# Output projection in sixteen half-depth passes, and scans by token half: a hybrid attention and delta-rule layer on one core

## The chip, the cores and the metric

The kernel runs on one core of one Trainium2 chip. The metric is the device time of one execution in microseconds. Several executions are timed and their median is used; one further execution is profiled, and all rows of the trace come from that one.

## What is computed

One layer over 1024 tokens of width 2048, in float32. The normalised input goes through one wide projection. Its columns feed eight heads of differential attention (A) and eight heads of a gated delta rule (B). The outputs of both are put side by side, multiplied by one more weight matrix, added to the input and normalised.

```python
h = rms_norm(x, norm_w)
proj = jnp.einsum('btd,dc->btc', h, w_in)
...
o_da = differential_attention(q1, q2, k1, k2, v_da, lam, rel_bias)
...
def step(S, inp):                      # one chunk of tokens of one head
    qc, kc, uc, wc, qkc, gc, glc = inp
    v_new = uc - jnp.einsum('bhcd,bhdv->bhcv', wc, S)
    o = (jnp.einsum('bhcd,bhdv->bhcv', qc * jnp.exp(gc)[..., None], S)
         + jnp.einsum('bhij,bhjv->bhiv', qkc, v_new))
    S = (S * jnp.exp(glc)[..., None, None]
         + jnp.einsum('bhcd,bhcv->bhdv', kc * jnp.exp(glc[..., None] - gc)[..., None], v_new))
    return S, o
...
mixed = jnp.concatenate([o_da, o_gdn], axis=-1)          # (1024, 2048)
x = x + jnp.einsum('btc,cd->btd', mixed, w_out)
return rms_norm(x, final_norm_w)
```

## The kernel before, in words

**Order of the work.** The program is written as coroutines ("lanes"), each of which yields one instruction at a time. A planner asks all lanes for their next instruction, works out with fixed costs when each could start, and emits the one that could start earliest; of equal ones the lane that stands first in the list wins. What comes out is one fixed order of instructions per engine and one fixed order of transfers on SyncE's queue (SP). A lane can also yield a condition, and then it stands still until the planner has emitted what the condition asks for. All instructions are issued by one helper, so the profile gives line 369 for nearly all of them (401 for transfers), and groups are told apart by tile names.

**Stages.** The input projection runs first, and attention beside it. When attention's last unit is done (`("attend", H - 1, 3)`), two things begin together: the scans of the delta rule, and the output projection.

**Scans.** There are 16: eight heads by two token halves of 512. `scan_loads` fetches six operands per scan (kT, qT, qk, Um in parts, vr, kh) into three sets of buffers; a set is loaded again when the scan that used it has ended. Two lanes, `scans(0)` and `scans(1)`, take the even and the odd heads. A scan has four steps of 128 tokens, each a chain through three engines: matmul with the state S, VectorE makes R, matmul with Um, ScalarE makes vn, matmul with kh, VectorE makes the next S. It uses four PSUM banks, `bka` and `bkb`, two for each lane. At its end it is normalised, turned, and stored to `mixed[1]` in DRAM. Before the change a lane takes a head's first half, then the same head's second half, then its next head.

**Output projection.** `mixed` has 16 blocks of 128 channels: 8 of attention (`mixed[0]`) and 8 of the scans (`mixed[1]`). The loop `out_products` goes over passes, a pass being one token half (four blocks of 128 tokens) by 512 output columns. Before the change there are eight, and each takes all 16 blocks of channels: for each pair of blocks j, and each block k and token block tb in it, three matmuls of 128x512 (operands are split into a high and a low part in fp32r, and high x high, low x high and high x low are summed). That is 192 matmuls into four PSUM banks. Even passes use the banks `prod` (two), `side` and `av`; odd passes use the scans' banks and ask for all scans to be done (`scans_done()`).

**Operands of the projection.** They live in the buffers of the input projection, which come free as its last products are issued (`FREE`). `out_weights` loads w_out 1 MB at a time (four blocks of channels by 512 columns) into `B11h` and `B11l` and splits it in two parts into the slots `RING_W`; `out_left` loads 1 MB of `mixed` at a time through `T1h` and splits it into the slots `RING_A`. For ScalarE and VectorE (or GpSimd) a part is one copy and one subtraction of 128x1024.

**Rows of the result.** `acc_loads` loads x in eight row blocks, three in tiles named `raw`, the fourth in `acc`; blocks 4 to 7 take the same four places when blocks 0 to 3 are stored (`("stored", n - 4)`). `collect_out` adds the four banks of a pass to them on VectorE. `half_row` normalises and stores a row block; it needs `fnw`, the final norm's weights, which `last_room` loads when all scans are done.

Of the kernel before, what the change touches and what calls it, by code (L numbers as in the profile page):

```python
# [11 lines left out]
F32 = mybir.dt.float32  # L12
# [11 lines left out]
D = 2048  # L24
H = 8
P = 128
# [440 lines left out]
@with_exitstack  # L467
def hybrid_trunk(ctx: ExitStack, tc: tile.TileContext, a, out):
    nc = tc.nc
    plan = Planner(tc, ("s_rest", "s_narrow", "s_blocks", "s_turn", "follow", "follow_b", "s_ts", "drain", "scores", "tails", "outputs", "s_norm", "s_scales", "weights", "s_nsum", "s_sums", "s_scale", "keys", "lead", "norms", "side_w", "products"))  # L470
    s_rest, s_narrow, s_blocks, s_turn, follow, follow_b, s_ts, drain, scores_, tails, outputs, s_norm, s_scales, weights_, s_nsum, s_sums, s_scale, keys, lead, norms, a_lane, main = plan.lanes
    pe, act, dve, pool = plan.engines
    dma = plan.dma

# [44 lines left out]
    done = set()  # L519
    box = {}  # L520

    def when(*keys):
        return lambda: all(k in done for k in keys)
# [30 lines left out]
    def bank_of(lane):  # L554
        return ps.tile([P, 512], F32, ("bka", "bkb")[lane], 2)
# [1017 lines left out]
    def scan_loads():  # L1573
        yield when(("attend", H - 1, 3))
        box["ast"].close()
        plan.margin = lambda: 0.0
        box["gst"] = ExitStack()
        gp = box["gp"] = rpool(box["gst"], "gp")
        for h0 in range(0, H, 2):
            for h, g in ((h0, 0), (h0 + 1, 0), (h0, 1), (h0 + 1, 1)):  # L1580
                yield when(("gq", h, g), ("gv", h, g))
                yield lambda: len(ring) < SETS or ring[-SETS][0]
                flag = [False]
                ring.append(flag)
                cs = slice(4 * g, 4 * g + 4)
                kT = gp.tile([P, 512], F32, "kT", SETS)
                dma(kT, kd[h][:, hsl(g)])
                qT = gp.tile([P, 512], F32, "qT", SETS)
                dma(qT, gq[h][:, hsl(g)])
                qk = gp.tile([P, 4, P], F32, "qk", SETS)  # L1590
                dma(qk, ed[h][:, cs])
                U = gp.tile([P, 4, P], F32, "Um", SETS)
                yield pool.memset(U[64:128, :, 0:64], 0.0)
                for s in range(2):
                    dma(U[64 * s:64 * s + 64, :, 64 * s:64 * s + 64], ud[h, cs, s].rearrange("c j i -> j c i"))
                dma(U[0:64, :, 64:128], u12d[h][:, cs])
                vr = gp.tile([P, 4, P], F32, "vr", SETS)
                dma(vr, gv[h][:, cs])
                kh = gp.tile([P, 4, P], F32, "kh", SETS)
                dma(kh, khd[h][:, cs])  # L1600
                ahead[h, g] = kT, qT, qk, U, vr, kh, flag

    def scans(lane):
        ends = None
        for h, g in [(h, g) for h in range(lane, H, 2) for g in range(2)]:
            ends = yield from scan(lane, h, g, ends)
        yield from ends

    def scan(lane, h, g, ends):
# [12 lines left out]
        o = vr  # L1622
        S = last_s.get(h)
        for k in range(4):
# [17 lines left out]
            if c < NT - 1:  # L1642
                p4 = bank_of(lane)
                yield pe.matmul(p4[:, :P], kh[:, k], vn, start=True, stop=True)
                Sn = gp.tile([P, P], F32, f"S{lane}", 2)
                if c:
                    yield dve.scalar_tensor_tensor(out=Sn, in0=S, scalar=egl[:, h, c:c + 1], in1=p4[:, :P],
                                                   op0=ALU.mult, op1=ALU.add)
                else:
                    yield dve.tensor_copy(Sn, p4[:, :P])  # L1650
                S = Sn
# [70 lines left out]


    wo_v = w_out.rearrange("(a p) d -> p a d", p=P)
    RAW_W, RAW_A = ("B11h", "B11l"), ("T1h",)
    RING_W = ("T2h", "T2l", "T3h", "T3l")
    RING_A = ("T1l", "B21h", "B21l", "T4h", "T4l", "B22h", "B22l", "x0", "x1")
    FREE = {n + e: LAST - 6 + i for i, (_, n) in enumerate(ORDER) for e in "hl"}
    PASSES = [(half, q) for half in range(2) for q in range(4)]
    NP = len(PASSES)  # L1730
    ops, used, acc = {}, set(), {}
    passed = [0]

    def scans_done():
        return all(("scan", h, g) in done for h in range(H) for g in range(2))
# [9 lines left out]
    def slot(tag, shape, dt):  # L1745
        if tag in FREE:
            yield lambda: issued[0] >= FREE[tag]
        else:
            yield lambda: "fp" in box
        return (hp if tag in FREE else box["fp"]).tile(shape, dt, tag)  # L1750

    def raw_rows(n, names, src):

        t = yield from slot(names[n % len(names)], [P, 4, 512], F32)
        dma(t, src)
        return t

    def parts(key, names, raw):

# [7 lines left out]
        ops[key] = t[:, 0], t[:, 1]  # L1767

    def out_weights():
        raws = {}  # L1770

        def fetch(n):
            if n < NP * 4:
                p, j = divmod(n, 4)
                q = PASSES[p][1]
                raws[n] = yield from raw_rows(n, RAW_W, wo_v[:, 4 * j:4 * j + 4, q * 512:(q + 1) * 512])

        for n in range(len(RAW_W)):
            yield from fetch(n)
        for n in range(NP * 4):  # L1780
            for i in range(2):
                yield from parts(("w", 2 * n + i), RING_W, raws[n][:, 2 * i:2 * i + 2])
            yield from fetch(n + len(RAW_W))

    def out_left():
        for n in range(8):
            half, j = divmod(n, 4)
            chunk, k = divmod(4 * j, NH)
            if chunk:
                yield when(*(("scan", k + i, half) for i in range(4)))  # L1790
            else:
                yield when(*(("attend", k + i, 2 * half + m) for i in range(4) for m in range(2)))
            raw = yield from raw_rows(n, RAW_A, mixed[chunk][:, k:k + 4, half * 512:(half + 1) * 512])
            for i in range(2):
                yield from parts(("a", 2 * n + i), RING_A, raw[:, 2 * i:2 * i + 2])

    def acc_loads():
        yield lambda: issued[0] >= LAST - 1
        for n in range(8):
            if n >= 4:  # L1800
                yield when(("stored", n - 4))
            if n % 4 < 3:
                t = wp.tile([P, D], F32, "raw", 3)
            else:
                yield lambda: "fp" in box
                t = box["fp"].tile([P, D], F32, "acc")
            dma(t, x[n * P:(n + 1) * P])
            acc[n] = t

    def out_products():  # L1810
        for p, (half, q) in enumerate(PASSES):
            if p % 2 == 0:
                yield when(("attend", H - 1, 3))
                yield lambda: drained[0] == LAST and side_free[0] and passed[0] >= p - 1
                pts = [wide(), wide(), ps.tile([P, 512], F32, "side"), ps.tile([P, 512], F32, "av")]
                side_free[0] = False
            else:
                yield lambda: scans_done() and passed[0] >= p - 1
                pts = [bank_of(i // 2) for i in range(4)]
            for j in range(8):  # L1820
                yield lambda: ("a", 8 * half + j) in ops and ("w", 8 * p + j) in ops
                (ah, al), (wh, wl) = ops["a", 8 * half + j], ops["w", 8 * p + j]
                for k in range(2):
                    for tb in range(4):
                        ts = slice(tb * P, (tb + 1) * P)
                        for m, (l, r) in enumerate(((ah, wh), (al, wh), (ah, wl))):
                            yield pe.matmul(pts[tb], l[:, k, ts], r[:, k], start=j + k + m == 0,
                                            stop=(j, k, m) == (7, 1, 2))
                        if j == 7 and k == 1:
                            drain.push(collect_out(p, half, q, tb, pts[tb]))  # L1830
                used.add(("w", 8 * p + j))
                if q == 3:
                    used.add(("a", 8 * half + j))

    def collect_out(p, half, q, tb, pt):
        c, o = divmod(q, 2)
        yield lambda: 4 * half + tb in acc
        t = acc[4 * half + tb][:, q * 512:(q + 1) * 512]
        yield dve.tensor_tensor(out=t, in0=t, in1=pt, op=ALU.add)
        if o:  # L1840
            norms.push(half_row(half, tb, c))
        if tb == 3:
            passed[0] += 1
            if p % 2 == 0:
                side_done()

    sums = {}
# [69 lines left out]
```

## Time and profile before

| | us |
|---|---|
| three runs | 2138.02, 2135.84, 2138.13 |
| median | 2138.02 |
| profiled execution | 2136.91 |
| its span, first to last instruction | 2135.2 |
| TensorE busy | 1958.1 |
| VectorE busy | 1521.3 |
| ScalarE busy | 1060.6 |
| GpSimd busy | 356.3 |
| mean granted TensorE clock | 0.959 of full speed |

The span is what the trace covers; the time of the same execution is 1.7 us longer. Busy times are sums of instruction durations as the trace has them. TensorE's matmuls are pipelined, so their durations overlap or include latency, and how many matmuls fit into a stretch is read from the starts. The weight loads of TensorE ("PEld") run beside its matmuls.

### The profile page before, as it was taken

To read this page: it belongs to the slowest core of one execution; us is meant where nothing else is said; L and a number is where in the kernel's file an instruction comes from. 1 tells how busy PE (TensorE), PEld (TensorE's weight loads), DVE (VectorE), ACT (ScalarE), POOL (GpSimd) and SP (SyncE) were. 2 spreads that over 40 slices of the span, in tenths; PEclk is the share of its full clock that TensorE was granted. 3 is DMA by queue.
4 is the path that set the end of the run, shared out by engine and by line. 5 is a ranking of instruction groups with operands and counts; after the bars stand their busy time and mean duration, and the time that the engine had idled before them with its cause. 6 is when DMAs were issued, how large, how long until landed. Compare 5 with 4: busy or idle time off the path is not lost.

```text
span 2135.2 us, 28911 instructions
## 1 busy us (share of the span) xinstructions
PE 1958.1 (92%) x10221; PEld 1206.0 (56%) x10221; DVE 1521.3 (71%) x2802; ACT 1060.6 (50%) x2261; POOL 356.3 (17%) x380
## 2 busy tenths in 40 slices
PE   3699999999997999998999998999989887999996
PEld 3544544444443445555655554555557675888885
DVE  6767977968998954889868797878984554334342
ACT  5654554643445334666656565656763432224122
POOL 5403113121112101111111120111220110000000
PEclk7699999999999999998999999999999998999998
DMA  8046666475465686446567545644357754236432
GB/s 239 5 113 144 123 149 172 119 181 157 94 84 65 114 185 158 109 105 161 150 131 143 99 115 115 133 121 107 103 218 228 213 175 157 99 120 224 168 99 79
DMA packets 234497, 292.28 MB, mean 137 GB/s; under 512 B 51744, under 2 KB 160496, under 8 KB 231920
## 3 DMA queue, kind: packets, MB, share of 16 engines
q1 hardware_dynamic: 234352, 290.43, 53.4%
q8 instruction: 81, 1.33, 0.3%
q14 instruction: 64, 0.52, 0.1%
HBM read 206.44 MB, written 85.50 MB: 137 GB/s over the span
## 4 chain that ended last, share of the span: by engine, by line
PE 68%; DVE 14%; DMA 8%; ACT 4%; issue 4%; POOL 2%; SPq 1%; POOLq 0%; ACTq 0%; DVEq 0%
PE prod L369 43%; PE bka L369 8%; PE bkb L369 8%; PE av L369 5%; PE side L369 4%; DVE wlo L369 2%; DMA raw<-in_w_in_dram 2%; DVE c L369 1%; DVE raw L369 1%; DVE A L369 1%; SPq L401 1%; ACT jkw L369 1%; DVE tmp L369 1%; DMA gq<-c 1%; DMA T1h<-mixed 1%
## 5 line engine op out<-in xcount | busy, mean ns | idle before, releaser
L369 PEld LDWEIGHTS <-whi 128*128 128x128 f16 x3680 | 360.3, 100 | 410.0 <-issue 41.8
L369 PEld LDWEIGHTS <-wlo 128*128 128x128 f16 x1840 | 184.1, 100 | 211.1 <-DVE wlo L369 20.4
L369 ACT ACTIVATE whi<-raw,sc 128x1024 f16<-128x1024 f32 x160 | 182.5, 1146 | 206.4 <-PE prod L369 111.6
L369 DVE SCALAR_TENSOR_TENSOR wlo<-raw,sc,whi 128x1024 f16<-128x1024 f32 x160 | 206.1, 1293 | 20.9 <-ACT whi L369 20.6
L369 ACT ACTIVATE jkw<-raw 128x1024 bf16<-128x1024 f32 x140 | 147.2, 1051 | 55.7 <-DVE raw L369 27.6
L369 POOL TENSOR_TENSOR sum<-raw 128x1024 f32<-128x1024 f32 x32 | 79.2, 2474 | 291.9 <-DVE wlo L369 248.1
L369 PE MATMUL prod<-T2h,wlo 128*128 128x512 f16 (+1 forms) x280 | 103.2, 370 | 7.9 <-DVE wlo L369 7.9
L369 PE MATMUL prod<-B11h,wlo 128*128 128x512 f16 (+1 forms) x280 | 104.3, 374 | 5.3 <-DVE wlo L369 5.3
L369 PE MATMUL prod<-B11h,whi 128*128 128x512 f16 (+1 forms) x280 | 104.3, 374 | 5.0 <-ACT whi L369 5.0
L369 DVE SCALAR_TENSOR_TENSOR wlo<-sum,sc,whi 128x1024 f16<-128x1024 f32 x64 | 82.1, 1283 | 35.1 <-ACT whi L369 33.8
L369 PE MATMUL prod<-T4h,whi 128*128 128x512 f16 x256 | 99.7, 389 | 7.8 <-DVE U L369 7.8
L369 PE MATMUL prod<-T2h,whi 128*128 128x512 f16 (+1 forms) x280 | 103.1, 369 | 2.6 <-ACT whi L369 2.6
L369 PE MATMUL prod<-B11l,whi 128*128 128x512 f16 (+1 forms) x280 | 104.0, 373 | 0.0
L369 PE MATMUL prod<-T3h,whi 128*128 128x512 f16 x256 | 97.5, 381 | 6.2 <-ACT q L369 6.2
L369 PE MATMUL prod<-T2l,whi 128*128 128x512 f16 (+1 forms) x280 | 103.1, 369 | 0.0
L369 PE MATMUL prod<-B21h,whi 128*128 128x512 f16 x256 | 97.8, 382 | 4.6 <-DVE V L369 4.6
L369 PE MATMUL prod<-T4l,whi 128*128 128x512 f16 x256 | 99.5, 389 | 0.0
L369 PE MATMUL prod<-T4h,wlo 128*128 128x512 f16 x256 | 99.4, 388 | 0.0
L369 PE MATMUL prod<-B21h,wlo 128*128 128x512 f16 x256 | 97.8, 382 | 0.0
L369 PE MATMUL prod<-T3l,whi 128*128 128x512 f16 x256 | 97.6, 381 | 0.0
L369 PE MATMUL prod<-B21l,whi 128*128 128x512 f16 x256 | 97.6, 381 | 0.0
L369 PE MATMUL prod<-T3h,wlo 128*128 128x512 f16 x256 | 97.3, 380 | 0.0
(579 smaller groups left out, 4890.8 us busy)
## 6 DMA issues: line engine op xcount, KB each, us to landing
raw<-in_w_in_dram SPq DMA_DIRECT2D x64, 1024.0 KB, 10.7
qst<-qd SPq DMA_DIRECT2D x256, 64.0 KB, 2.5
B11h<-in_w_out_dram SPq DMA_DIRECT2D x16, 1024.0 KB, 5.2
B11l<-in_w_out_dram SPq DMA_DIRECT2D x16, 1024.0 KB, 5.2
xt<-in_x_dram SPq DMA_DIRECT2D x8, 1024.0 KB, 7.0
qd<-c SPq DMA_DIRECT2D x32, 256.0 KB, 3.0
T1h<-mixed SPq DMA_DIRECT2D x8, 1024.0 KB, 5.5
raw<-in_x_dram SPq DMA_DIRECT2D x6, 1024.0 KB, 8.6
```

The source lines that it names most:

```text
L369: op.fn(*op.args, **op.kw)
L401: (self.nc.scalar if d.bulk else self.nc.sync).dma_start(out=d.out, in_=d.in_)
```

## The change

The projection gets sixteen passes instead of eight: a pass is now a token half, half of the channels (`part` 0 is attention's, `part` 1 the scans') and 512 columns, 96 matmuls. The order is first token half with part 0 in four passes, then part 1, then the second token half alike. Each pass is added to the row blocks, so there are twice as many additions. A pass takes whichever set of banks is free: the first set, or the scans' banks when all scans are done; there is one coroutine of drains, in order of the passes. The scans run all heads' first token halves and then all heads' second ones; the state between the halves of a head is kept in a tile of its own (`Sh{h}`). Weight and token loads share the two 1 MB buffers `B11h` and `B11l`: a weight load is only started when both are free, until the last token operand has been split. The splits of the weights are in a new lane (`splits`). There are three weight slots instead of four and eight token slots instead of nine, and `T1h` holds the fourth row block.

```diff
-        for h0 in range(0, H, 2):
-            for h, g in ((h0, 0), (h0 + 1, 0), (h0, 1), (h0 + 1, 1)):
+        for g in range(2):
+            for h in range(H):
...
-        for h, g in [(h, g) for h in range(lane, H, 2) for g in range(2)]:
+        for h, g in [(h, g) for g in range(2) for h in range(lane, H, 2)]:
...
-                Sn = gp.tile([P, P], F32, f"S{lane}", 2)
+                Sn = gp.tile([P, P], F32, f"Sh{h}") if k == 3 else gp.tile([P, P], F32, f"S{lane}", 2)
...
-    RAW_W, RAW_A = ("B11h", "B11l"), ("T1h",)
-    RING_W = ("T2h", "T2l", "T3h", "T3l")
-    RING_A = ("T1l", "B21h", "B21l", "T4h", "T4l", "B22h", "B22l", "x0", "x1")
+    RAW = ("B11h", "B11l")
+    RING_W = ("T2h", "T2l", "T3h")
+    RING_A = ("T3l", "T1l", "B21h", "B21l", "T4h", "T4l", "B22h", "B22l")
+    RING_X = "T1h"
...
-    PASSES = [(half, q) for half in range(2) for q in range(4)]
+    PASSES = [(half, part, q) for half in range(2) for part in range(2) for q in range(4)]
...
-    def raw_rows(n, names, src):
-
-        t = yield from slot(names[n % len(names)], [P, 4, 512], F32)
+    def raw_rows(src, keep=0):
+
+        yield lambda: len(raw_free) > keep or bool(raw_free) and "left" in done
+        tag = min(raw_free)
+        raw_free.remove(tag)
+        t = yield from slot(tag, [P, 4, 512], F32)
         dma(t, src)
-        return t
+        return t, tag
...
     def out_weights():
...
+        for n in range(NP * 2):
+            p, i = divmod(n, 2)
+            _, part, q = PASSES[p]
+            j = 2 * part + i
+            raw, tag = yield from raw_rows(wo_v[:, 4 * j:4 * j + 4, q * 512:(q + 1) * 512], 1)
+            out_splits.push(both("w", n, RING_W, raw, tag))
+            yield lambda: len(out_splits.tasks) < 2
+
+    def both(kind, n, names, raw, tag):
+        for i in range(2):
+            yield from parts((kind, 2 * n + i), names, raw[:, 2 * i:2 * i + 2])
+        raw_free.add(tag)
 
     def out_left():
...
+            if n:
+                yield lambda: ("a", 2 * n - 1) in ops
+            yield lambda: 2 * n < len(RING_A) or ("a", 2 * n + 1 - len(RING_A)) in used
+            raw, tag = yield from raw_rows(mixed[chunk][:, k:k + 4, half * 512:(half + 1) * 512])
+            yield from both("a", n, RING_A, raw, tag)
+        done.add("left")
...
     def acc_loads():
...
-                yield lambda: "fp" in box
-                t = box["fp"].tile([P, D], F32, "acc")
+                t = yield from slot(RING_X, [P, D], F32)
...
     def out_products():
-        for p, (half, q) in enumerate(PASSES):
-            if p % 2 == 0:
-                yield when(("attend", H - 1, 3))
-                yield lambda: drained[0] == LAST and side_free[0] and passed[0] >= p - 1
+        owner = [-1, -1]
+        yield when(("attend", H - 1, 3))
+        yield lambda: drained[0] == LAST
+        for p, (half, part, q) in enumerate(PASSES):
+            def free(s):
+                return owner[s] < passed[0] and (scans_done() if s else side_free[0])
+            yield lambda: free(0) or free(1)
+            s = 0 if free(0) else 1
+            owner[s] = p
+            if s:
+                pts = [bank_of(i // 2) for i in range(4)]
+            else:
                 pts = [wide(), wide(), ps.tile([P, 512], F32, "side"), ps.tile([P, 512], F32, "av")]
                 side_free[0] = False
-            else:
-                yield lambda: scans_done() and passed[0] >= p - 1
-                pts = [bank_of(i // 2) for i in range(4)]
-            for j in range(8):
...
+            for j in range(4):
+                ka, kw = ("a", 8 * half + 4 * part + j), ("w", 4 * p + j)
...
     def collect_out(s, half, part, q, tb, pt):
...
-        if o:
+        if o and part:
             norms.push(half_row(half, tb, c))
```

## Rows read from the trace of the kernel before

**Rows 1.** Page, the span in 40 slices of 53.4 us: TensorE busy tenths, granted clock.

```profile
PE   3699999999997999998999998999989887999996
PEclk7699999999999999998999999999999998999998
```

**Rows 2.** By stage: length, busy us (count) PE, PEld, DVE, ACT, POOL; clock.

```profile
1600.50:1812.40 211.90, 177.06 (x976) 146.23 (x975) 113.17 (x396) 72.87 (x259) 24.88 (x31) 0.90 0.62 194
...
1812.40:2117.10 304.70, 304.70 (x1346) 252.31 (x1345) 107.60 (x110) 82.06 (x90) 2.19 (x4) 1.00 0.37 125
...
2117.10:2135.20 18.10, 0.71 (x4) 0.25 (x2) 7.57 (x15) 8.29 (x12) 2.17 (x4) 0.61 0.59 232
...
1610.00:1637.00 27.00, 27.00 (x173) 24.07 (x173) 15.34 (x48) 10.11 (x36) 1.31 (x2) 1.00 0.67 210
...
1700.00:1722.00 22.00, 21.84 (x130) 19.48 (x131) 12.32 (x42) 7.89 (x28) 3.45 (x3) 0.92 0.64 193
```

**Rows 3.** The same table, of instructions on the banks bka alone.

```profile
1610.00:1637.00 27.00, 11.01 (x63) 10.31 (x64) 6.76 (x22) 2.87 (x9) 1.00 0.67 210
1700.00:1722.00 22.00, 8.94 (x46) 8.09 (x46) 5.55 (x17) 2.50 (x8) 0.92 0.64 193
```

**Rows 4.** The same table, of instructions on the banks bkb alone.

```profile
1610.00:1637.00 27.00, 8.31 (x44) 7.26 (x44) 4.62 (x15) 2.23 (x7) 1.00 0.67 210
1700.00:1722.00 22.00, 7.57 (x39) 6.76 (x40) 4.39 (x13) 1.62 (x5) 0.92 0.64 193
```

**Rows 5.** Timeline of TensorE: start, us, instruction, count; pass 0 and scans.

```profile
1600.53 2.91 PE L369 MATMUL prod<-T2h,T1l 128*128 128x512 f32 x6
...
1605.69 0.63 PE L369 MATMUL prod<-T2h,T1l 128*128 128x512 f32 x2
...
1631.91 0.38 PE L369 MATMUL bka<-R,Um 128*128 128x128 f32 x2
1632.13 0.39 PE L369 MATMUL bkb<-S,kT 128*128 128x128 f32 x2
...
1636.94 0.60 PE L369 MATMUL bka<-ident,vr 128*128 128x128 f32 x4
1637.38 0.39 PE L369 MATMUL bka<-S,kT 128*128 128x128 f32 x2
```

**Rows 6.** Timeline of SyncE's queue: scan results stored, their loads.

```profile
1638.36 0.33 SPq L401 DMA_DIRECT2D mixed<-zt  x1
...
1692.11 0.37 SPq L401 DMA_DIRECT2D T1h<-mixed  x1
...
1784.51 0.37 SPq L401 DMA_DIRECT2D T1h<-mixed  x1
...
1800.75 0.32 SPq L401 DMA_DIRECT2D mixed<-zt  x1
```

**Rows 7.** TensorE's waits from 1600.5 to 1812.4: total us, times, longest.

```profile
PE bkb L369 <- DVE R L369: 6.0, 10, 1.0
PE bkb L369 <- DVE vr L369: 5.4, 5, 2.0
...
PE bkb L369 <- issue: 0.2, 1, 0.2
```

**Rows 8.** Instructions on the weight buffer B11h: duration ns min/median/max.

```profile
L369 ACT ACTIVATE T2h<-B11h x16: 1040/1061/1067, 1576.2 to 2079.8; 128x1024 fp32r<-128x1024 f32 x16
...
L369 DVE TENSOR_TENSOR T2h<-B11h,T2h x15: 1220/1226/1227, 1609.7 to 2080.9; 128x1024 fp32r<-128x1024 f32 x15
...
DMA to landing us min/median/max: 5.0/5.2/12.4
```

**Rows 9.** Timeline of VectorE after the first token half: additions into row blocks.

```profile
1941.73 1.37 DVE L369 TENSOR_TENSOR raw<-raw,bka 128x512 f32<-128x512 f32 x2
...
1985.25 1.37 DVE L369 TENSOR_TENSOR raw<-raw,prod 128x512 f32<-128x512 f32 x2 [1.08 <-PE prod L369]
...
1993.32 0.69 DVE L369 TENSOR_TENSOR acc<-acc,av 128x512 f32<-128x512 f32 x1 [3.71 <-DMA acc<-in_x_dram]
```

More of the change, by code (lines that the diff above doesn't have):

```diff
@@ L469, in hybrid_trunk @@
     nc = tc.nc
-    plan = Planner(tc, ("s_rest", "s_narrow", "s_blocks", "s_turn", "follow", "follow_b", "s_ts", "drain", "scores", "tails", "outputs", "s_norm", "s_scales", "weights", "s_nsum", "s_sums", "s_scale", "keys", "lead", "norms", "side_w", "products"))
-    s_rest, s_narrow, s_blocks, s_turn, follow, follow_b, s_ts, drain, scores_, tails, outputs, s_norm, s_scales, weights_, s_nsum, s_sums, s_scale, keys, lead, norms, a_lane, main = plan.lanes
+    plan = Planner(tc, ("s_rest", "s_narrow", "s_blocks", "s_turn", "follow", "follow_b", "s_ts", "drain", "scores", "tails", "outputs", "s_norm", "s_scales", "weights", "s_nsum", "s_sums", "s_scale", "splits", "keys", "lead", "norms", "side_w", "products"))
+    s_rest, s_narrow, s_blocks, s_turn, follow, follow_b, s_ts, drain, scores_, tails, outputs, s_norm, s_scales, weights_, s_nsum, s_sums, s_scale, out_splits, keys, lead, norms, a_lane, main = plan.lanes
     pe, act, dve, pool = plan.engines
@@ L1724, in hybrid_trunk @@
     wo_v = w_out.rearrange("(a p) d -> p a d", p=P)
-    RAW_W, RAW_A = ("B11h", "B11l"), ("T1h",)
-    RING_W = ("T2h", "T2l", "T3h", "T3l")
-    RING_A = ("T1l", "B21h", "B21l", "T4h", "T4l", "B22h", "B22l", "x0", "x1")
+    RAW = ("B11h", "B11l")
+    RING_W = ("T2h", "T2l", "T3h")
+    RING_A = ("T3l", "T1l", "B21h", "B21l", "T4h", "T4l", "B22h", "B22l")
+    RING_X = "T1h"
     FREE = {n + e: LAST - 6 + i for i, (_, n) in enumerate(ORDER) for e in "hl"}
-    PASSES = [(half, q) for half in range(2) for q in range(4)]
+    PASSES = [(half, part, q) for half in range(2) for part in range(2) for q in range(4)]
     NP = len(PASSES)
     ops, used, acc = {}, set(), {}
+    raw_free = set(RAW)
     passed = [0]
@@ L1769, in out_weights @@
     def out_weights():
[L1770 to L1783, printed above, removed]
+        for n in range(NP * 2):
[9 more added lines that the diff above has]
+        raw_free.add(tag)
     def out_left():
@@ L1792, in out_left @@
                 yield when(*(("attend", k + i, 2 * half + m) for i in range(4) for m in range(2)))
-            raw = yield from raw_rows(n, RAW_A, mixed[chunk][:, k:k + 4, half * 512:(half + 1) * 512])
-            for i in range(2):
-                yield from parts(("a", 2 * n + i), RING_A, raw[:, 2 * i:2 * i + 2])
+            if n:
[4 more added lines that the diff above has]
+        done.add("left")
     def acc_loads():
@@ L1810, in out_products @@
     def out_products():
-        for p, (half, q) in enumerate(PASSES):
-            if p % 2 == 0:
-                yield when(("attend", H - 1, 3))
-                yield lambda: drained[0] == LAST and side_free[0] and passed[0] >= p - 1
+        owner = [-1, -1]
[10 more added lines that the diff above has]
+            else:
                 pts = [wide(), wide(), ps.tile([P, 512], F32, "side"), ps.tile([P, 512], F32, "av")]
                 side_free[0] = False
-            else:
-                yield lambda: scans_done() and passed[0] >= p - 1
-                pts = [bank_of(i // 2) for i in range(4)]
-            for j in range(8):
-                yield lambda: ("a", 8 * half + j) in ops and ("w", 8 * p + j) in ops
-                (ah, al), (wh, wl) = ops["a", 8 * half + j], ops["w", 8 * p + j]
+            for j in range(4):
+                ka, kw = ("a", 8 * half + 4 * part + j), ("w", 4 * p + j)
+                yield lambda: ka in ops and kw in ops
+                (ah, al), (wh, wl) = ops[ka], ops[kw]
                 for k in range(2):
@@ L1827, in out_products, with collect_out @@
                             yield pe.matmul(pts[tb], l[:, k, ts], r[:, k], start=j + k + m == 0,
[L1828 to L1831, printed above, removed]
+                                            stop=(j, k, m) == (3, 1, 2))
+                        if j == 3 and k == 1:
+                            drain.push(collect_out(s, half, part, q, tb, pts[tb]))
+                used.add(kw)
                 if q == 3:
-                    used.add(("a", 8 * half + j))
-    def collect_out(p, half, q, tb, pt):
+                    used.add(ka)
+    def collect_out(s, half, part, q, tb, pt):
         c, o = divmod(q, 2)
@@ L1843, in collect_out @@
             passed[0] += 1
-            if p % 2 == 0:
+            if not s:
                 side_done()
```

## The prediction

> **What bounds the kernel now.** I read the page's forty slices first [rows 1]. TensorE is almost always busy and at full clock until slice 29. Then come about four slices at 7 and 8 tenths, with the clock at 8 and 9, and after them a stretch without a hole. So the change can only win in those slices, between attention's last matmul and the start of the long output stretch, and the next view is the table by stage [rows 2]. It cuts the end at three points. From 1600.5 to 1812.4 us the scans run together with pass 0 of the projection. From 1812.4 to 2117.1 passes 1 to 7 run alone, 1344 products in 304.7 us, which is 0.2267 us each, with TensorE busy throughout. The last 18.1 us are the final norm and store.
>
> In the middle stage the kernel issues 976 TensorE instructions: 192 are pass 0, and 784 are the scans, 49 for each of the 16. What they need at full clock I take from starts, not from busy time: two scan instructions start 0.22 us apart from the next two, and four transposes take 0.44 us, so 0.11 us each [rows 5]. That is 784 x 0.11 = 86.2 us and 192 x 0.2267 = 43.5 us, together 129.8 us in a stage of 211.9 us. **82.1 us of TensorE time are lost there**, partly as idle and partly as half clock (mean granted clock 0.90).
>
> Why they are lost is in the timelines. Pass 0 has products until 1637; then its second half needs heads 0 to 3 of the first token half, whose load leaves only at 1692.1, and the other four heads follow about 90 us later [rows 6]. Pass 1 asks for all scans to be done. Between these, TensorE has only the scans' own chains (matmul, VectorE, matmul, ScalarE, matmul, VectorE), and the list of waits shows what that costs: thirteen rows of the two scan banks, 27.0 us in all, mostly for R, vn and vr [rows 7]. The rest is half clock and the waits of pass 0 itself.
>
> **The change, part by part.** *Passes.* The products stay 1536 and the weight and token loads stay 32 and 8 of 1 MB. Passes 0 to 3 now need only attention's heads of the first token half, which are there at 1600.5. Passes 4 to 7 need the scans of the first half, and these now come first for all heads, so they are the first eight. Two stretches of before show what a stage with both kinds of work does [rows 2 to 4]. From 1610 to 1637 TensorE issued 173 instructions, 63 and 44 of them on the scan banks, so 66 products: 66 x 0.2267 + 107 x 0.11 = 26.7 us of work in 27.0. From 1700 to 1722 there are 45 products and 85 scan instructions, 19.6 us of work in 22.0 at a clock of 0.92, which began with a wait. Together 2.7 us of 49 are lost, 5.5%. At 107/27 and 85/22 instructions per us a scan of 49 takes 12.5 us, so 16 last 200 us; alone they needed 162.4/15 = 10.8 us each [rows 6]. The stretch costs the scans little, and the mixed products (111 in 49 us, 2.27 per us) come on top.
>
> Is there always a product? By 1750, 149 us at 2.27 per us make 338, less than the 384 of passes 0 to 3. The eighth scan ends near 1638 + 7 x 12.5 = 1726, and with store, load and split its operands are there by about 1740. So nothing waits there.
>
> *What stays lost.* The start at half clock: the first 12 products take 5.2 us instead of 2.7 [rows 5], 2.4 us. The mixed stage: 5.5% of 200 us, 11 us (bounds 2 and 22, the two stretches' own shares). I take the mean since the stage will hold both quiet and disturbed scans. The gap between two passes of the one slot is inside it, because the four banks are drained 0.69 us apiece [rows 9] and scan matmuls stand between.
>
> *Half the work per pass at the half-way point.* This is a new wait. The drains of pass 8 need x rows 512 to 1023, which are loaded into the row buffers when rows 0 to 511 are normalised and stored. Before, the last drain of the first token half began at 1941.7, and the fourth new row block was usable at 1993.3, where VectorE waited 3.71 us for the load: 51.6 us [rows 9]. Then a pass of 43.5 us and the next slot covered it. Now pass 10 takes pass 8's banks 43.5 us after pass 7 ends, and its first use of the fourth bank comes some 2 us later. It waits about 6 us, and about 3 us go for half clock behind it, as at 1600.5: 9 us (bounds 0, if rows are stored faster, and 20). Queued behind that drain on VectorE are the weight splits, so the weight feed stands still too; its slots are full by then.
>
> *Weights.* One weight load is in flight while the other buffer is kept for token operands, and there are three split slots for four. A load lands in 5.2 us (12.4 at worst) and is split by two ScalarE copies of 1.06 and two VectorE subtractions of 1.23 [rows 8]: with the second copy under the first subtraction, 5.2 + 1.06 + 2 x 1.23 = 8.7, with issue and hops some 9.5 us. It feeds 48 products, 10.9 us alone and 21 us when mixed. So it holds, with 1.4 us to spare where TensorE runs alone; I leave 3 us for the time around pass 8, when stores, x rows and the last token operands share the DMA engines (bounds 0 and 15).
>
> *At no cost.* 32 more VectorE adds of 0.69 us, 22 us, lie in VectorE's idle time (113 of 212 and 108 of 305 us busy [rows 2]); without that cover they would cost 22 us. The state kept per head replaces a ring of two and adds no instruction. The fourth row block is loaded into T1h as soon as that is free and no longer after the scans; else every fourth drain of a pass would wait for them. Less weight work lies beside attention's last units, and I give that nothing.
>
> **Sum.** 2135.2 - 82.1 + 2.4 + 11 + 9 + 3 = 2078.5 us of span. A second way: by 1610 there are 31 products (12 by 1605.7, then one per 0.2267 us), the scans end at 1810 with 453 more; 1052 are left, 238.5 us, then 12 us of the two waits and 18.1 of tail: 2078.6. The profiled execution took 1.7 us more than its span, and the median of the runs is 1.1 us above it: **2081 us**.
>
> **Rule against rows.** Busy time says less is to be had: 177 of 211.9 us leave 35. The Trainium skill (Perfetto Trace Analysis, Identifying the Most-Contended Engine) says that matmul busy time misleads and that the busy share of weight loads should be read instead. Here that share is 146.2/211.9 = 69.0%, against 82.8% in the full stage, so TensorE would be 83% used and 35.4 us free, not 82.1: a span of 2125. I keep the count, since the two mixed stretches really hold 26.7 and 19.6 us of such work in 27 and 22.
>
> **Rivals.**
> *Late scans hold the products (12%).* If TensorE starts nothing behind a matmul that waits, a scan matmul that waits for R or for a late load stops the products too. For it: Um, kT and vr wait on one queue, and the order is written by a planner with fixed costs. Against it: 0.3 us lost in the first mixed stretch. If all 27.0 us of scan waits stay on top [rows 7], 2108. The Trainium skill (TensorE: Matmul & The Clock Gate, Part 3) states the same strict order for matmuls.
> *The weight feed limits the mixed stage (8%).* If a load waits in SP's queue behind a scan's store and lands at the worst 12.4 us, a cycle is 26 us instead of 21; then 200 us hold 369 products and not 453: 84 x 0.2267 = 19 us, 2100.
> *The free time is 35 us by weight loads (4%).* 2128.
> *No mixing (4%).* If the order puts products behind the scans all the same, only the pass boundaries change: 2138.
> *Slower (6%).* Scans slowed by products beyond a point. Rows 0 to 511 can only be stored once all scans are done (the last norm's weights go where the scan tiles were), so products end at pass 8, 864 of them; with the scans that fills TensorE to 1883. From the scans' end it then takes 52 us until pass 8 is drained, 130.6 us for passes 10 to 15, 18.1 and 2.8: 203.5. That passes 2142 when the scans end after 1939, so from 20.6 us a scan on; each further us costs 16. At 22 us, 2161. Against it: 12.5 us measured with products beside them.
>
> **How the numbers follow.** The forecast has 66%; its own range is 2060 (mixed loss 2, no other wait) to 2100 (mixed 22, the two waits 20). The range goes down to 2056 for a shorter end of attention, and up to 2116 to take in the first two rivals. 0.2% are 4.3 us, about what this kernel's timing can tell. Faster: 66 + 12 + 8 + 4 = 90%; the same 4%; slower 6%.
>
> **What would show it.** Right: products through the whole scan stage at about 2.3 per us and a clock near 1.0; the last scan stored near 1810; some 1050 products after it; one hole of some 9 us about two passes after the first token half is drained; matmuls ending near 2060, then 18 us. Wrong: scan cadence over 15 us, holes before products that wait for a split, or waits for scan operands that come back in the list with the same 27 us.

## The result, and the profile after

The changed kernel takes 2071.8 us in the median of four runs (2066.8 to 2082.3), the kernel before 2136.9 on the same chip: 65 us less. The ratio of the runs is 0.970 (95% interval 0.966 to 0.974), which is 63 us. The forecast of 2081 us was right in sign and size. It is 9 us above the measured median; by the ratio, which allows for this chip's own time of the kernel before (0.9703 x 2138.0 = 2074.5), it is some 6 us too high.

The first profile caught an execution of 2082.3 us. I took a second one of the same kernel (label after_again below, 2077.0 us). The stores of attention show where the two differ: the first profile is already 5 to 6 us later here, before the part that the change is about has begun. Timeline of SyncE's queue, the last two stores of attention, first the first profile, then the second:

```profile
1592.26 0.33 SPq L401 DMA_DIRECT2D mixed<-gt  x1
1605.81 0.32 SPq L401 DMA_DIRECT2D mixed<-gt  x1
```

```profile
1586.54 0.33 SPq L401 DMA_DIRECT2D mixed<-gt  x1
1600.81 0.32 SPq L401 DMA_DIRECT2D mixed<-gt  x1
```

So I measure each profile from the start of pass 0 to the end of the matmuls, taken as 1.36 us after the start of the last group of six. The kernel before needs 517.1 us for that (1600.5 to 2117.65), the changed one 458.1 and 457.9 us in its two profiles. This **distance** hardly moved in the two kernels that were profiled twice (0.2 us here, 0.1 us for e4_rows below), and the runs below are compared by it as well as by their ratio. The other kernels have one profile each, so how far theirs would move is not known. The distance leaves out what happens before pass 0: by it 59 us were won, by the ratio 63.

The forty slices of the first profile (TensorE busy, granted clock), against [rows 1]: the dent in slices 30 to 34 (counted from 1) is gone. Slice 31 (about 1560 to 1612 us) is at 8, and most of it is attention's end; slice 38, at about 1925 to 1975 us, is new.

```profile
PE   3699999999998899998999999899998999999896
PEclk7699999999999999998999999999999999999998
```

The table by stage (length, busy us and count of PE, PEld, DVE, ACT, POOL, granted clock, DMA share, GB/s), cut at the start of pass 0, the last scan's store and the last matmuls, against [rows 2]:

```profile
1604.95:1841.97 237.02, 230.61 (x1382) 200.40 (x1382) 149.31 (x439) 95.17 (x282) 32.81 (x34) 0.99 0.66 213
1841.97:2063.00 221.03, 215.19 (x941) 177.54 (x939) 88.49 (x99) 61.41 (x71) 5.67 (x5) 0.98 0.40 139
2063.00:2080.60 17.60, 0.22 (x1) 0.00 (x0) 7.08 (x14) 7.80 (x11) 2.16 (x4) 0.59 0.60 238
```

The scan stage now holds 1382 TensorE instructions in place of 976. Without the 784 of the scans 598 products are left (before: 192). By the prediction's own prices (0.2267 us a product, 86.2 us for all scans) that is 598 x 0.2267 + 86.2 = 221.8 us of work in 237.0 us, 15.2 lost. Behind it are 938 products, 212.6 us in 221.0, 8.4 lost. Together 23.6 us are lost, where by the same count the kernel before loses 82.7 (348.2 + 86.2 of 517.1): 59 us came from there.

TensorE's waits over the same two stages (total us, times, longest), the first six of nine rows, against [rows 7]:

```profile
PE av L369 <- DVE T1h L369: 5.8, 1, 5.8
PE av L369 <- ACT oT L369: 2.6, 1, 2.6
PE bka L369 <- DMA qT<-gq: 2.5, 1, 2.5
PE bkb L369 <- ACT vn L369: 1.6, 3, 1.0
PE bka L369 <- ACT vn L369: 0.9, 1, 0.9
PE bkb L369 <- DMA vr<-gv: 0.5, 1, 0.5
```

The scan banks' waits (`bka`, `bkb`; three short rows are not shown) fell from 27.0 to 6.4 us. The wait for `oT` ended at 1604.76, just before pass 0, and lies outside the distance. The longest single wait is new, and it is the hole that was forecast. Timeline of TensorE at the hole, and of VectorE from the first token half's last additions to it, against [rows 9]:

```profile
1932.56 1.65 PE L369 MATMUL av<-T2l,T3l 128*128 128x512 f32 x3 [5.84 <-DVE T1h L369]
1934.01 2.72 PE L369 MATMUL prod<-T2l,T3l 128*128 128x512 f32 x6
```

```profile
1882.06 0.68 DVE L369 TENSOR_TENSOR T1h<-T1h,bkb 128x512 f32<-128x512 f32 x1
...
1931.82 0.69 DVE L369 TENSOR_TENSOR T1h<-T1h,av 128x512 f32<-128x512 f32 x1 [4.78 <-DMA T1h<-in_x_dram]
```

From the last addition to the fourth block (1882.06) to its first addition for the second half (1931.82) it takes 49.8 us: normalise, store, load x again. A pass takes 43.5 us. Six matmuls of 128x512 then take 2.72 us where six take 1.52 at full clock (2.4 GHz): the clock has fallen in the hole. The mean granted clock from 1932.56 to 1938.00 is 0.63, and from 1938.00 on it is 1.00 again.

The scans' stores and the token loads, against [rows 6]:

```profile
1647.24 0.33 SPq L401 DMA_DIRECT2D mixed<-zt  x1
...
1741.44 0.33 SPq L401 DMA_DIRECT2D mixed<-zt  x1
1745.54 0.37 SPq L401 DMA_DIRECT2D B11l<-mixed  x1
...
1841.97 0.32 SPq L401 DMA_DIRECT2D mixed<-zt  x1
```

The eighth store is at 1741.4, its load leaves 4.1 us later, and no product waits for it. From the first to the sixteenth store it takes 194.7 us, 13.0 a scan.

One loss does not show in the list of waits. SyncE sends a weight load at 1733.4 and the next only at 1775.2, because token loads take both 1 MB buffers in between. ScalarE's part of the first split of that load ends at 1782.16, and the first product with it starts at 1782.93. From 1776.8 to 1782.9 TensorE has no product, only 36 scan instructions, 4.0 us of work in 6.1. It is the longest stretch without products in the scan stage, and it comes back in after_again (6.3 us). The scan instructions stand before the product in the fixed order, so the waits are put down to them.

### The profile page after: what moved, and what is told of

Same layout as the page of the kernel before. It is cut to its first block, busy times and chain, and to the rows that moved or that the text cites. A ratio compares the mean times of both kernels' runs of the same rounds, so it can differ in the third digit from the quotient of the medians.

```text
span 2080.6 us, 28925 instructions
## 1 busy us (share of the span) xinstructions
PE 1922.2 (92%) x10221; PEld 1185.3 (57%) x10221; DVE 1533.1 (74%) x2831; ACT 1058.7 (51%) x2261; POOL 362.2 (17%) x383
## 4 chain that ended last, share of the span: by engine, by line
PE 65%; DVE 14%; DMA 10%; issue 4%; ACT 4%; POOL 2%; SPq 1%; POOLq 0%; DVEq 0%; ACTq 0%
PE prod L369 43%; PE bka L369 6%; PE bkb L369 6%; PE av L369 5%; PE side L369 4%; DVE wlo L369 2%; DMA raw<-in_w_in_dram 2%; DVE c L369 2%; DVE raw L369 1%; SPq L401 1%; DVE A L369 1%; ACT jkw L369 1%; DVE tmp L369 1%; ACT whi L369 1%; DMA gq<-c 1%
## 5 line engine op out<-in xcount | busy, mean ns | idle before, releaser
L369 DVE SCALAR_TENSOR_TENSOR wlo<-raw,sc,whi 128x1024 f16<-128x1024 f32 x160 | 206.1, 1293 | 20.9 <-ACT whi L369 20.6
L369 DVE SCALAR_TENSOR_TENSOR wlo<-sum,sc,whi 128x1024 f16<-128x1024 f32 x64 | 82.1, 1283 | 34.1 <-ACT whi L369 32.9
L369 PE MATMUL prod<-T1l,whi 128*128 128x512 f16 x256 | 97.4, 380 | 0.0
```

The lines of the kernel that those rows point to most:

```text
L369: op.fn(*op.args, **op.kw)
```

## The experiments

The theory is the prediction's: TensorE lost 82 us for want of products beside the scans, and the passes of half the depth put them there. Rivals were that the new order of scans does it alone, that the buffers or the shorter passes at the boundaries do it, and that the part before the scans does it. "After" is the changed kernel.

**e1_passes_only: after, with the old order of the scans.**

```diff
-        for g in range(2):
-            for h in range(H):
+        for h0 in range(0, H, 2):
+            for h, g in ((h0, 0), (h0 + 1, 0), (h0, 1), (h0 + 1, 1)):
...
```

The same order stands in `scans`, and the state goes back to the two tiles `S{lane}`.

> Sixteen passes as in the change, but the scans in the old order (a head's two token halves behind each other). Theory (the gain is products put into TensorE's free time beside the scans, and the scan order only decides when passes 4 to 7 may go on): passes 0 to 3 and half of pass 4, some 430 products, fit beside the scans, then products run out near the 14th scan and about 12 us are lost: 2084 us. Rival (passes alone do it, the order is worth nothing): 2072. Rival (the order is the gain): 2137.

Measured 2100.2 us, ratio 0.982 (0.980 to 0.984), distance 479.6. The passes alone give some 60% of the gain, and the order is worth 1.2% or 25 us on top of them by the ratio, 22 us by the distance. That is twice what I had expected: the theory's 2084 us was 16 us too low, and both rivals were further off. The same 80 us of both (e1, then after_again) show where:

```profile
1760.00:1840.00 80.00, 67.77 (x358) 54.64 (x358) 46.90 (x146) 29.96 (x90) 10.78 (x12) 0.91 0.57 182
```

```profile
1760.00:1840.00 80.00, 78.87 (x466) 68.11 (x465) 50.30 (x154) 34.24 (x99) 16.24 (x14) 1.00 0.61 198
```

108 TensorE instructions are missing, 24 us at a product's 0.2267. In e1 the tokens of heads 4 to 7 are loaded only at 1813.5 (1745.5 in after). The number of products that fit was forecast well, 423 against some 430, but they are used up by 1778.5, near the 11th scan and not the 14th. From there to 1820.1, for 41.6 us, TensorE has only the scans again; the mean clock of the 80 us is 0.91.

**e2_scan_order_only: before, with the new order of the scans** (the same lines the other way).

> The kernel before with the new scan order alone; still eight passes of all channels, and pass 1 waits for all scans. Theory: the second half of pass 0 can run after the eighth scan and no longer at the end, which saves some 10 us where it stood alone and gives a few back as slower scans: 2130 us. Rival (the order is the gain): near 2072. Rival (order without effect): 2137.

Measured 2133.0, ratio 0.997 (0.996 to 0.999), distance 513.2. The order by itself is worth 6 us by the ratio and 4 by the distance, near the theory's 2130 and far from either rival.

**e3_gate: after, but from pass 2 on a pass waits for all scans.**

```diff
-            yield lambda: free(0) or free(1)
+            yield lambda: (p < 2 or scans_done()) and (free(0) or free(1))
```

> The changed kernel, but from pass 2 on every pass waits until all scans are done: the mixing is undone, and the sixteen passes, the buffers, the doubled additions and the scan order stay. Theory: the time goes back to that of the kernel before, 2137 us (2130 to 2142). Rival (buffers, drains or the end of attention bring the gain): it stays near 2072 to 2090.

Measured 2133.1, ratio 0.998 (0.996 to 0.999), distance 515.4. Everything else of the change is in it: the sixteen passes, the new order of the scans, the shared buffers, the doubled additions. Passes 0 and 1 run beside the scans, 192 products as in the kernel before; only the products beside the later scans are missing, and the gain is gone. The old dent is back (stages of e3):

```profile
1680.00:1720.00 40.00, 32.39 (x179) 26.24 (x179) 23.71 (x91) 16.66 (x62) 7.60 (x9) 0.87 0.71 218
1720.00:1760.00 40.00, 31.98 (x196) 26.11 (x196) 24.46 (x92) 16.82 (x65) 6.50 (x8) 0.96 0.74 230
1760.00:1800.81 40.81, 30.25 (x145) 24.15 (x146) 20.75 (x81) 11.72 (x48) 5.43 (x7) 0.74 0.31 96
```

So mixing is the gain. The scans end at 1800.8 here, 10.8 us each; in after 13.0. With products beside them they take 2.2 us more a scan, and still the distance is 57 us shorter than e3's.

**e4_rows: after, with places of their own for row blocks 4 to 6;** block 7 takes the place of block 0, the first to be stored.

```diff
-            if n >= 4:
-                yield when(("stored", n - 4))
-            if n % 4 < 3:
+            if n < 3:
                 t = wp.tile([P, D], F32, "raw", 3)
-            else:
+            elif n == 3:
                 t = yield from slot(RING_X, [P, D], F32)
+            elif n < 7:
+                yield lambda: "fp" in box
+                t = box["fp"].tile([P, D], F32, f"row{n}")
+            else:
+                yield when(("stored", 0))
+                t = wp.tile([P, D], F32, "raw", 3)
```

> The changed kernel with places of their own for row blocks 4 to 6 (in the room freed by the scans), so that only block 7 waits for a stored block, the first of them. Theory (the hole before pass 10 is the wait for the places of blocks 0 to 3): the hole of 5.8 us and some 2.6 us of half clock behind it go: 8 us less than the changed kernel on the same chip, 2063 us. Rival (VectorE's queue or the crowd of transfers makes the hole): no difference, 2072.

Measured 2065.2 us, ratio 0.966 (0.963 to 0.968), distance 449.0. The hole is gone: from the last scan's store to the last matmul (the second row) TensorE has no idle time and full clock.

```profile
1599.98:1835.83 235.85, 230.64 (x1382) 200.44 (x1381) 149.52 (x439) 95.04 (x282) 33.65 (x34) 0.99 0.67 214
1835.83:2048.94 213.11, 213.11 (x941) 176.24 (x939) 88.84 (x99) 61.36 (x71) 6.60 (x5) 1.00 0.41 145
```

From the last scan's store to the end of the matmuls the two profiles of after need 221.1 and 220.7 us, e4 213.1. So the hole had cost 8.0 and 7.6 us: the starts show about 6.0 and 5.3 of standstill (the list puts the waits at 5.8 and 5.1) and 2.0 and 2.3 of lower clock behind it. The other 1.2 us of the 9.0 between the distances (458.0 and 449.0) lie beside the scans, 235.9 us against 237.0 and 237.2, and what they come from was not followed up. By the distance this version beats both kernels; by the ratio its lead over after is 0.5%, and the two intervals touch.

**after_again: the changed kernel once more.**

> The changed kernel once more, unaltered, beside the kernel before. My reading of its first trace is that the profiled execution, 2082.3 us, is its slowest, 10 us above its median, and that 7.6 us of this were lost before attention's end, in a part whose instructions stand in the same order in both kernels. Then a second profile must show the second last store of attention (before 1584.8 us, changed 1592.3) back near 1585, the start of pass 0 near 1598 to 1600, the last group of matmuls near 2051 to 2055, and the same losses behind it: about 15 us in the scan stage and 6 us at the wait for row blocks 4 to 7. Rival: the change itself slows the part before, through loads that it issues earlier; then the second profile shows 1592 again and about 2080. Median expected 2071, 2067 to 2075.

Measured 2077.1 us, ratio 0.970 (0.968 to 0.973); the kernel before took 2140.6 on this chip. The second last store of attention is at 1586.5 and pass 0 starts at 1599.9, as expected, and the losses behind it are the same: 15.4 us in the scan stage, and a wait of 5.1 us for the row blocks. The last group of matmuls starts at 2056.4, 1.4 us later than expected, and the median lies 6 us above what I expected; the ratio is the same.

**e5_two_slots: after, with two slots for split weights.**

```diff
-    RING_W = ("T2h", "T2l", "T3h")
+    RING_W = ("T2h", "T2l")
```

> The changed kernel with two slots for split weights in place of three. The trace of the changed kernel shows no product that waits for a split; the prediction gave 3 us, from 1.4 us of slack per load of 48 products. By that reckoning two slots just hold: a slot comes free, 2.3 us later it is split again, the other comes free after 5.4 us and is split at 7.7, the next load lands some 6 us later at 13.7, its first split is there at 16.0, and TensorE needs it at 16.3. So where TensorE runs alone it holds by 0.3 us, and only loads that land late cost something: 2072 to 2086, most likely 2077. Rival: the feed is already at its limit with three slots, and one slot less costs some 2 us per load alone, 19 loads after the scans: 2100 or more. Second rival: there is much more room than I worked out, and nothing changes: 2070 to 2073.

Measured 2086.0, ratio 0.975 (0.972 to 0.978), 0.45% or 10 us more than after, 9 us by the medians and by the distance (466.8). That is in the upper half of the theory's 0 to 14 us, counted from after, and far from the rival's 28 us and more. The only waits of products for a split stand at one place, the first at 1899.2 us:

```profile
PE bka L369 <- ACT T2h L369: 1.7, 1, 1.7
...
PE bka L369 <- DVE T2h L369: 0.5, 1, 0.5
```

There SyncE sends a token load at 1880.4 and the next weight load only at 1891.7. The planner also put 27 fewer products (1355 - 784 = 571) beside the scans. Where only weights are loaded no product waits for a split, so two slots hold there; three cover the place where tokens and weights want the same two 1 MB buffers.

**e6_late_weights: before, with the weight loads held until attention's second last unit;** in `out_weights`:

```diff
+        yield when(("attend", H - 1, 2))
```

> The kernel before, with the loads of the output weights held until attention's second last unit is done. It asks whether the work on weights and tokens for the projection, beside attention's last units, makes these longer. In the kernel before, the last two stores of attention lie 16.7 us apart, in the changed one 13.6, and VectorE's own operations take two to three times as long there while GpSimd subtracts (V<-c,V 2.18 us, else 0.7 to 0.9). If that is the cause, the spacing falls to 13 to 14 us, and pass 0 starts with its first weights late by a load and a split, 5 to 10 us: median 2138 to 2146. If the spacing stays above 15.5 us, the splits are not the cause, and the 3 us are scatter between executions.

Measured 2137.2, ratio 0.999 (0.997 to 1.000), distance 514.7. The spacing is 18.6 us, not 13 to 14: by the test that I had set, the splits are not the cause. But the second last store itself came earlier (31.4 us behind the one before it, else 33.0), so the spacing was a poor measure. Chosen after the result, and so weaker, is TensorE's wait for `al` in the last unit, in before, e6 and after_again:

```profile
PE side L369 <- DVE al L369: 4.4, 3, 2.0
...
PE side L369 <- DVE al L369: 2.0, 2, 1.3
...
PE side L369 <- DVE al L369: 1.5, 2, 0.8
```

It fell, but the time did not change beyond its interval.

**e7_vector_splits: before, with all subtractions of the splits on VectorE.**

```diff
-        yield Choice(*(e.tensor_tensor(out=t[:, 1], in0=raw, in1=f32(t[:, 0]), op=ALU.subtract) for e in (dve, pool)),
-                     lean=0.7)
+        yield dve.tensor_tensor(out=t[:, 1], in0=raw, in1=f32(t[:, 0]), op=ALU.subtract)
```

> The kernel before, with every subtraction of the splits for the output projection on VectorE, none on GpSimd. If GpSimd's subtractions stretch VectorE's work at attention's end, then VectorE's operations there have their usual length (V<-c,V under 1 us), the last two stores of attention lie 13 to 15 us apart in place of 16.7, although VectorE now does nine subtractions of 1.23 us more, and the median is 2133 to 2137. Rival: the stretching is not from GpSimd, the added 11 us of VectorE work lie on attention's chain, and the median is 2138 to 2148.

Measured 2135.9, ratio 0.997 (0.996 to 0.999), distance 513.5. VectorE's operations have their usual length again, so GpSimd had stretched them. First the kernel before at attention's end, VectorE and then GpSimd, then VectorE in e7:

```profile
1584.69 2.18 DVE L369 SCALAR_TENSOR_TENSOR V<-c,V 128x512 f32<-128x512 f32 x1
...
1589.58 0.68 DVE L369 TENSOR_TENSOR al<-side,ah 128x512 fp32r<-128x512 f32 x1
1590.32 2.65 DVE L369 TENSOR_TENSOR T4h<-T1h,T4h 128x1024 fp32r<-128x1024 f32 x1
```

```profile
1583.95 2.37 POOL L369 TENSOR_TENSOR T3h<-B11l,T3h 128x1024 fp32r<-128x1024 f32 x1 [1.28 <-ACT T3h L369]
1586.28 2.82 POOL L369 TENSOR_TENSOR T3l<-B11l,T3l 128x1024 fp32r<-128x1024 f32 x1
1589.06 2.83 POOL L369 TENSOR_TENSOR B21l<-T1h,B21l 128x1024 fp32r<-128x1024 f32 x1
```

```profile
1589.61 0.68 DVE L369 SCALAR_TENSOR_TENSOR V<-c,V 128x512 f32<-128x512 f32 x1
...
1594.94 1.22 DVE L369 TENSOR_TENSOR T4h<-T1h,T4h 128x1024 fp32r<-128x1024 f32 x1
```

The expected spacing of 13 to 15 us did not come, though: it is 18.6, and the wait for `al` is still 3.2 us; VectorE now has the subtractions between its own work, which may be why. The distance is 3.6 us shorter than before's, so most of what was gained lies behind the start of pass 0.

**e4_again and e8_rows_vector: e4_rows once more, and e4_rows with e7's edit.**

> The kernel with row blocks 4 to 6 in places of their own, once more, beside the next run. Its first profile ran from the start of pass 0 (1600.0) to the end of the matmuls (2048.9) in 449.0 us, the changed kernel in 458.0 and 458.1 us (two profiles). If the hole is worth these 9 us, the same 449 us (448 to 451) come back, wherever the start of pass 0 falls by scatter (1598 to 1607). Ratio to the kernel before 0.966 (0.963 to 0.969).

> The same kernel with every subtraction of the splits on VectorE, none on GpSimd. The kernel before gained 0.26% (0.13 to 0.38) by this, 3.1 us of it in the scan stage. If GpSimd's subtractions hold the scans' VectorE work up, which the longer VectorE instructions beside them suggest, this kernel gains as much: ratio 0.9635 (0.961 to 0.966), with 447 us or less from the start of pass 0 to the end of the matmuls. Rival: with products beside the scans TensorE is the limit of that stage and the scans wait for it, not for VectorE; then nothing changes, ratio 0.966 and 449 us. Second rival: the 10 to 15 subtractions that come to VectorE fill it, and the stage gets longer: 451 us or more.

e4_again: 2069.4, ratio 0.968 (0.965 to 0.970), distance 449.1, as expected. e8: 2076.2, ratio 0.971 (0.968 to 0.974), distance 456.3. The theory's 447 us did not come. e8 lost 7 of the 9 us that e4 had won, as its second rival had said in size, but at a place that neither theory nor rival had named. The two intervals of the ratio overlap; the distances, of one profile here and two of e4, do not. TensorE's timeline and SyncE's queue in e8:

```profile
1898.19 3.33 PE L369 MATMUL prod<-T2l,B21h 128*128 128x512 f32 x6 [5.02 <-ACT T2l L369]
```

```profile
1869.26 0.38 SPq L401 DMA_DIRECT2D B11h<-in_w_out_dram  x1
1869.69 1.45 SPq L401 DMA_DIRECT2D B11l<-mixed  x1
1879.92 0.37 SPq L401 DMA_DIRECT2D B11h<-mixed  x1
...
1887.27 0.38 SPq L401 DMA_DIRECT2D B11l<-in_w_out_dram  x1
```

With another order of splits both 1 MB buffers held tokens, no weights were loaded for 18 us, and a product waited 5.0 us; six matmuls then took 3.33 us. By the starts this place cost 8.3 us, and beside the scans e8 loses 1 us less than e4. It is the place of e5's waits too.

## Why the prediction was right, step by step

*What is lost (82.1 us).* Right, and by the mechanism given: e3 keeps everything but the mixing and gains 0.2%. Of the 82.7 us 23.6 remain, against 2.4 + 11 + 9 + 3 = 25.4 forecast. The distance was forecast at 460.4 us, taken to the same end, and is 458.0. That the sum came out so close is in part luck: beside the scans 1.8 us more were lost than forecast, behind them 3.6 us less (8.4 instead of 12).

*The start (2.4) and the mixed stage (11 us, bounds 2 and 22).* Together 15.2 against 13.4. The share was nearly right, the time table was not: "16 last 200 us" put the last scan at 1810, 209 us after the start of pass 0, and it came 237 us after it. The step began 16 scans of 12.5 us at 1610; but the first scan stores only 42 us after the start of pass 0 (38 in the kernel before), the other fifteen follow, and each took 13.0 us. It did little harm, because TensorE was busy all the longer: 598 products went into the stage at 2.5 per us, against 484 at 2.3, and 938 instead of 1052 were left. So two of the signs given for being right, the last scan near 1810 and some 1050 products behind it, did not show.

*"So nothing waits there."* Right: the eighth scan's operands were late by the same shift (load at 1745.5 instead of a split by 1740), and passes 0 to 3 covered it. e1 shows what it costs if they don't: 22 to 25 us.

*The hole before the fourth bank of pass 10 (9 us: 6 of wait, 3 of half clock).* Right in place and mechanism, and in size within 1 us or so: 7.6 and 8.0 us against e4, of which about 2 are half clock.

*Weights (3 us).* Placed wrong: around pass 8 no product of after waits for a split. The feed does run dry once, but beside the scans, where the 41.8 us between two weight loads leave 6.1 us without a product; with 4.0 us of scan work in them, some 2 us are lost there, and they are part of the 15.2. The slack around pass 8 is small all the same: one slot less costs 9 or 10 us (e5), part of it there, and another order of the splits 7 us (e8).

*At no cost.* The 32 additions were hidden: VectorE is busy 149 of 237 us, and e3 has them too and is no slower than before. "Less weight work lies beside attention's last units, and I give that nothing" was probably wrong by about 3 us. TensorE's wait for `al` there fell from 4.4 to 1.5 us in both profiles of after, and by the ratio after gained some 4 us more than by the distance, on both chips. The start of pass 0 itself scatters too much to show it (1598.5 to 1608.2 in the profiles). e7 shows one part of the cause, GpSimd's subtractions stretching VectorE's; but without them the wait is still 3.2 us, e6 did not gain clear of its interval, and how much the rest of the splits add was not separated. With the 2.4 us of the distance this covers most of the 6 us by which the forecast was too high. The tail is no part of it: from the end of the matmuls it is 17.5 us in both kernels, and the 18.1 us of the prediction start 0.55 us before that end.

*The rivals.* Late scans holding the products would have left 27.0 us of scan waits; 6.4 are left. No mixing (2138) is what e3 shows where the mixing is taken out, 2133. The weight feed, which was to cost 19 us beside the scans, cost some 2. The scans stayed far below the 20.6 us each from which the change would have been slower; the price named there for 22 us a scan should be 2165 us by the prediction's own sum (1610 + 352 + 203.5), not 2161. The free time of 35 us by weight loads was too small: 59 us were won, and the stage now shows a weight-load share of 200.4/237.0 = 84.5%, above the 82.8% that was taken for full. The Trainium skill (Perfetto Trace Analysis, Identifying the Most-Contended Engine) says to judge TensorE's headroom by that share, beside the share of the peak arithmetic, and not by matmul busy time. In this stage the trace agrees that matmul busy time misleads, but the weight-load share, read against the full stage as the prediction read it, gave the same 35 us. Read against 100% it gives 211.9 - 146.2 = 66 us, but then the full stage, in which TensorE never waits, would have 17% to spare. The count of instructions by their starts did better.

## What to carry over

Where a chain through several engines leaves TensorE idle, count the instructions in the stage and price each by the spacing of starts: here this told the free time as 82 us, of which 59 were won, while the busy share told 35. Independent work must be in reach at the moment of want, so cut it by what it needs first (here attention's half of the channels), and order the producers so that the next piece is complete before the first is used up. Then follow each buffer that now turns over in half the time: the wait for the row blocks cost 8 us, and giving three of them places of their own got these back. And a list without a wait is no proof that a feed keeps up: look for stretches without the work itself.

## What was unexpected in the hardware

While GpSimd subtracts 128x1024 tiles in SBUF, a VectorE operation with two SBUF inputs does not slow down, it stands still until GpSimd is done. V<-c,V starts at 1584.69, GpSimd's subtraction ends at 1586.32, and V ends at 1586.87, 0.55 us later (it needs 0.68 in e7). T4h<-T1h,T4h starts at 1590.32, GpSimd ends at 1591.89, T4h at 1592.97, 1.08 us later (1.22 in e7). But al<-side,ah, which reads one input from PSUM, takes its usual 0.68 us at 1589.58 in the middle of a GpSimd subtraction. It is so in the whole trace of the kernel before: the seven operations of 512 or 1024 columns with two inputs in SBUF that its timeline shows singly and that start inside a GpSimd operation of 128x1024, at least 0.3 us before its end, all end 0.55 or 1.08 us (within 0.01) behind it, and 21 with an input from PSUM keep their usual length within 3%. The Trainium skill (SBUF — State Buffer, SBUF: two separate sides) states this: the two engines share a pair of ports under an exclusive lock, which a VectorE operation with two SBUF inputs needs against a GpSimd operation that reads SBUF. The trace agrees.
